# Decay rows inside the second score matmul, and compressed values at full height, in a two-layer hybrid decoder trunk

## The chip, the cores and the metric

The kernel runs on one core of a Trainium2 chip. The metric is device time in microseconds (us) for one execution. Three runs of the kernel before gave 987.95, 988.15 and 989.37 us; the median is 988.15.

## What is computed

Two layers on 512 tokens of width 1024, all in float32. Each layer normalises its input, projects it, and lets four token mixers work side by side: sparse attention (NSA: compressed, selected and window keys), pooling, a short convolution, and forgetting attention (Fox). Each result is gated, projected back to 1024, weighted by a merge gate, summed, and sent through an output projection onto the residual. The two parts that the change touches:

```python
# Fox: a score gets the difference of two cumulated log decays
logf = jax.nn.log_sigmoid(f_logit + f_bias)
c = jnp.cumsum(logf, axis=1)
s = jnp.einsum('bqhd,bkhd->bhqk', q_blk, k)
s = s + jnp.transpose(c_blk, (0, 2, 1))[..., None] - c_keys[:, :, None, :]
p = masked_softmax(s, (kpos[None, :] <= t[:, None])[None, None])
o = jnp.einsum('bhqk,bkhd->bqhd', p, v)
# NSA: attention over 31 compressed keys and values, four heads
s = jnp.einsum('bqhd,bnd->bhqn', q_blk, kc)
p_c = masked_softmax(s, (cmp_end[None, :] <= t[:, None])[None, None])
o_cmp = jnp.einsum('bhqn,bnd->bqhd', p_c, vc)
```

## The kernel before, in words

**Number format.** TensorE (PE) works on float32r, a rounded float32. Each operand is split into a high and a low part (`split`), and a product is three matmuls (high x high, high x low, low x high). ScalarE (ACT) makes the high part, VectorE (DVE) the low one.

**Dense products.** `dense` makes one 128-row output tile with 24 matmuls of 128x512. Its weights come from a list of 80 tiles per layer that `Stream` loads and splits ahead of their use. Each result leaves through a generator in `bg`, which is pumped one step after every second matmul.

**Score blocks.** `Unit.S(qt)` makes the scores of 128 queries against 128, 256, 384 or 512 keys. A head's query tile holds 64 rows of high part and 64 of low part (`q_stacks`); its key tiles hold the high part twice and the low part twice, one above the other (`k_stacks`, lines 284 to 295). So the first matmul (L565) gives (q high + q low) x k high, and the second (L566) (q high + q low) x k low. For the Fox heads a third one (L570) adds the decays. It has 32 rows, of which four are filled: keys hold the cumulated decay's high part, its low part, -1 and -1 (`state["cb"][0]`, in the buffer ropeC); queries hold 1, 1, the high part and the low part (`state["cb"][1]`, in ropeS). Each head has its own 32 rows, head h the rows from 32h. `decay` makes both tiles from `gz`.

**The rest of a block.** VectorE takes the minimum (the scores are negated; L573), ACT the exponential (L575), VectorE scales; `Unit.T` transposes on PE (L594), `split` takes that out to pth and ptl, and `Unit.PV` multiplies by the values (L615). For the first unit of each NSA head, `cmp_pv` opens the output with the compressed part: the transposed compressed probabilities of all four heads lie in one tile, 32 rows per head, and each head's matmul (L453) takes its 32 rows of it and of the compressed values `vc`, twice (high and low probabilities).

**Order.** Twelve units: for each of four heads a selected and a window unit (0 to 7), then four Fox heads (8 to 11). The loop runs 4 x 12 + 9 = 57 steps. A unit's four score blocks stand on its steps 0 to 3, its transposes on 4, 6 and 7, its value products on 7, 9 and 10. After each step `FILL` = 7 matmuls of the dense filler (Fox queries and keys, convolution, pooling, first merge gates) are put in. The framework then orders each engine's instructions; on the chip each engine takes its own in that order.

**Buffers.** The split queries and keys of a layer lie in 20 buffers called st: 4 of the NSA queries, 4 of the NSA keys, 4 of the Fox queries, 8 of the Fox keys. Weights use some of them before. Two PSUM buffers hold scores (ps_s), two hold transposes (ps_pt), one holds the output (ps_o).

Of the kernel before, what the change touches and what calls it, by code (L numbers as in the profile page):

```python
# [11 lines left out]
ALU = mybir.AluOpType  # L12
# [12 lines left out]
GATES = [(0, 0), (2, 0), (0, 1), (2, 1), (1, 0), (3, 0), (1, 1), (3, 1)]  # L25
BIG = 1e30
SWAP = [(i + 8) % 16 if i < 16 else i for i in range(32)]

# columns of the constant array
C_ID, C_TRI, C_MZ, C_CM, C_VAL, C_WINV, C_FIX, C_KCC, C_KCS, C_ROW = (  # L30
    0, 128, 256, 768, 896, 897, 899, 931, 963, 995)
NCONST = C_ROW + 6
# columns of the per-layer parameter array
P_B1, P_B2K, P_PSC, P_CW, P_POS, P_PW, P_W2K, P_W2V = 0, 2, 3, 5, 11, 43, 299, 427
# [5 lines left out]
def trunk_kernel(ctx: ExitStack, tc: tile.TileContext, xT, w_all, par_all, const, gains, rope, outT):  # L40
# [23 lines left out]
    def split(hi, lo, src, scale=None):  # L64
        """hi + lo = src (* scale), each in float32r."""
        if scale is None:
            ACT.activation(hi, src, AF.Copy)  # L67
            DVE.tensor_tensor(lo, src, f32(hi), ALU.subtract)  # L68
        else:
            ACT.activation(hi, src, AF.Copy, scale=scale)  # L70
            DVE.scalar_tensor_tensor(lo, src, scale, f32(hi), op0=ALU.mult, op1=ALU.subtract)  # L71

    # ---------------------------------------------------------------- constants
    cst = cpool.tile([128, NCONST], F32, name="cst")
# [5 lines left out]

    # ---------------------------------------------------------------- weights
    class Stream:
# [27 lines left out]
        def split(self, upto):  # L110
            while self.done <= min(upto, self.n - 1):
# [5 lines left out]
                if i == 2 or hid:  # L117
                    # slots that the stacks of q and k need only later
                    q = [sb([128, T], "st", 20, F32R) for _ in range(4)]
                    if hid:  # L120
                        for n in range(4):
                            v = q[n].rearrange("p (c two j) -> p c two j", two=2, j=128)
                            split(v[:, :, 0, :], v[:, :, 1, :],
                                  r[:, n * 256:n * 256 + 256].rearrange("p (c j) -> p c j", j=128))
                        self.parts[i] = q, None
                    else:
                        for n in range(2):
                            split(q[n], q[2 + n], r[:, n * 512:n * 512 + 512])
                        self.parts[i] = tuple(
                            [q[2 * j + k // 4][:, k % 4 * 128:k % 4 * 128 + 128] for k in range(8)]  # L130
                            for j in range(2))
                    self.load()
                    continue
# [27 lines left out]

    # ---------------------------------------------------------------- norm statistics
    def sum_squares(n, first, last):
        """add the squares gathered so far to the sums over the features"""
        if first:
            state["ssq"] = psum("o", 1)
        p, sq = state["ssq"], state["sq"]
        for tt in range(n // 128):
            PE.matmul(p[:, tt:tt + 1], sq[:, tt * 128:tt * 128 + 128], onesf[:, 0:1],  # L169
                      start=(first and tt == 0), stop=(last and tt == n // 128 - 1))  # L170
# [33 lines left out]

    # ---------------------------------------------------------------- dense products
    bg = []
# [15 lines left out]
    def dense(rhs, evac, tok=slice(0, T)):  # L222
        """one 128-row output tile: 8 contraction tiles, 3 passes"""
        i, (wh, wl) = ws.take()
# [27 lines left out]

    # ---------------------------------------------------------------- evacuations
    def scaled(acc):
# [26 lines left out]

    def k_stacks(dst, t):
        for o in (0, 64):
# [8 lines left out]
            yield  # L292
            ACT.activation(lo[e:e + 64], f32(lo[o:o + 64]), AF.Copy)
            dst.append((h, lo))
            yield

    # ---------------------------------------------------------------- compressed keys and values
    def ev_kcvc(acc):
# [81 lines left out]
    def cmp_v():  # L380
# [16 lines left out]
        yield  # L397
        vc = sb([128, 128], "vc", 1, F32R)
        split(vc[:, 0:64], vc[:, 64:128], r)
        state["vc"] = vc  # L400
# [49 lines left out]
    def cmp_pv(O, h):  # L450
        r = slice(32 * h, 32 * h + 32)
        for j, part in enumerate(state["pc"]):
            PE.matmul(O, state["vc"][r, :], part[r, :], start=(j == 0), stop=False,  # L453
                      tile_position=(32 * h, 0))

    # ---------------------------------------------------------------- values, gates of heads, decay
    def v_group(l):
# [90 lines left out]

    # ---------------------------------------------------------------- attention
    class Unit:  # L550
# [6 lines left out]
        def S(self, qt):  # L557
# [5 lines left out]
            s = psum("s", 2)  # L563
            qs = q[:, qt * 128:qt * 128 + 128]
            PE.matmul(s[:, :n], qs, kh[:, :n], start=True, stop=False)  # L565
            PE.matmul(s[:, :n], qs, kl[:, :n], start=False, stop=(self.head is None))  # L566
            if self.head is not None:
                r = slice(32 * self.head, 32 * self.head + 32)
                ck, cq = state["cb"]
                PE.matmul(s[:, :n], cq[r, qt * 128:qt * 128 + 128], ck[r, :n], start=False, stop=True,  # L570
                          tile_position=(32 * self.head, 0))
            nm, sm = sb([128, 1], "nm", 4), sb([128, 1], "sm", 4)
# [71 lines left out]

    # ---------------------------------------------------------------- conv and pool branches
    def ev_conv(kind, f):
# [79 lines left out]

    # ---------------------------------------------------------------- merge and output projection
    def ev_merge(i):
        # sigmoid(z) = (1 + tanh(z / 2)) / 2: tanh shares a function table with exp
        def g(acc):  # L730
            t = scaled(acc)
            state["sig"][i] = t
            yield
            ACT.activation(t, t, AF.Tanh, scale=0.5)  # L734
            yield
        return g
# [25 lines left out]

    # ================================================================ program
    nc.gpsimd.dma_start(ng, gains)
# [35 lines left out]
    for l in range(L):  # L800
        state["l"] = l
        state["gate"], state["y"], state["sig"] = {}, {}, {}
        Cp, Sp = sb([128, T], "ropeC", 1), sb([128, T], "ropeS", 1)
        nc.sync.dma_start(Cp, rope[0])
        nc.sync.dma_start(Sp, rope[1])
        rhs = (xh, xl)
        # first projections; the evacuation waits for the norm's statistics
        g0 = dense(rhs, ev_kcvc)
# [6 lines left out]
        run(g0)  # L815
        state["nk"], state["nq"], state["fq"], state["fk"] = [], [], [], []

        def ev_kskw(acc):
# [12 lines left out]
        def ev_fk(acc):  # L831
            t = scaled(acc)
            yield
            yield from k_stacks(state["fk"], t)

# [27 lines left out]

        # attention, with the remaining projections between its steps
        units = []
# [38 lines left out]
        for s in range(4 * len(units) + 9):  # L904
            for kind in ("PV", "T", "S"):
                for u in (s // 4 - 3, s // 4 - 2, s // 4 - 1, s // 4):
                    b = plan[kind].get(s - 4 * u)
                    if 0 <= u < len(units) and b is not None:
                        if kind == "S" and b == 0:
                            if u == 8:  # L910
                                while len(state["fk"]) < 4:
                                    next(fill)
                        getattr(units[u], kind)(b)
            for _ in range(FILL):
# [3 lines left out]

        # merge gates, branch projections
        ah, al = [], []  # L920
# [9 lines left out]

        # output projection and residual
        if l + 1 < L:
# [14 lines left out]

    # last layer: the tokens in two halves, so that the first one's norm and stores overlap
    xn = []
# [34 lines left out]

# [1 line left out]
def _constants(np):  # L986
# [11 lines left out]
    c[:, C_VAL] = p >= 31  # L998
    row = p % 32
    for j, v in enumerate(((0, 1), (2, -1), (1, 1), (2, 1), (0, 1), (3, 1))):  # L1000
        c[row == v[0], C_ROW + j] = v[1]
# [26 lines left out]
def _layout(np, a):  # L1028
# [8 lines left out]
    for l in range(L):  # L1037
# [7 lines left out]
        tiles = [feat(kv(0) + kv(1)), feat(kv(2) + kv(4)), feat(run(0)), feat(run(128))]  # L1045
        vc = kv(3) + kv(5) + list(range(2188, 2444)) + list(range(640, 652)) + list(range(2444, 2448))
        wv = w[:, vc].reshape(4, 2, 128, 400).transpose(0, 2, 1, 3).reshape(4, 128, 800)
# [29 lines left out]
        p[:, P_B2V:P_B2V + 64] = a["cmp_b2"][l, 1][None, :]  # L1077
        p[:, P_FB:P_FB + 4] = a["fox_f_bias"][l][None, :]
    return {"xT": a["x"][0].T, "w_all": w_all, "par": par, "const": c, "gains": ng, "rope": rope}
# [22 lines left out]
```

## Time and profile before

| | |
|---|---|
| median of three runs | 988.15 us (987.95 to 989.37) |
| the profiled execution, from its first to its last instruction | 987.6 us |
| PE busy | 970.9 us, 98%, 4824 matmuls |
| DVE, ACT, POOL busy | 653.6, 452.8, 12.9 us |
| granted TensorE clock, mean | 0.998 of full speed (2.4 GHz) |
| attention, first layer | about 110 to 262 us; its Fox scores 219 to 259 us |
| attention, second layer | about 590 to 748 us; its Fox scores 700 to 746 us |

The page shows one execution; it gives that one's span and no separate time. The span is 0.55 us below the median of the timed runs. Busy time counts an instruction's whole span. Matmuls overlap: their ends are modelled, and the distance between two starts is what the second one had to wait for the first.

### The profile page before, as it was taken

Reading aid. Unit: us, or ns where it says so; the run is one execution under the profiler, and the core shown is the slowest. Engines: PE = TensorE matmul, PEld = TensorE weight load, DVE = VectorE, ACT = ScalarE, POOL = GpSimd, SP = SyncE. Lnnn points to the kernel's source line nnn. Section 1 sums busy time; section 2 is a strip of 40 time slices with the busy share of each in tenths; the row PEclk is TensorE's granted clock in tenths of the full one; section 3 lists DMA queues with packets and bytes.
Section 4 is the critical chain, followed back from the end, with each engine's and each line's share of the span. In section 5 each row is a group of like instructions: output and inputs, shape, how many; then the busy total and the mean of one; then the engine's idle time right before and its main releaser. Section 6 shows DMA issues by size and latency. Waiting matters only on the chain.

```text
span 987.6 us, 12730 instructions
## 1 busy us (share of the span) xinstructions
PE 970.9 (98%) x4824; PEld 815.5 (83%) x4824; DVE 653.6 (66%) x1295; ACT 452.8 (46%) x800; POOL 12.9 (1%) x21
## 2 busy tenths in 40 slices
PE   7999999999999999999999999999999999999996
PEld 5988888887788888888889888888877888888896
DVE  6695699887675554446668549989668555454565
ACT  6294575555432322233427537555454323232363
POOL 0000000000000000000100000000000000000001
PEclk9999999999999999999999999999999999999999
DMA  6253221121213322334424322112111332323553
GB/s 257 77 172 105 86 85 62 47 98 32 75 65 111 103 95 98 97 117 169 166 67 160 124 89 83 65 65 64 65 43 43 107 103 89 107 86 107 171 193 128
DMA packets 31837, 100.62 MB, mean 102 GB/s; under 512 B 3600, under 2 KB 5664, under 8 KB 31776
## 3 DMA queue, kind: packets, MB, share of 16 engines
q1 hardware_dynamic: 30240, 96.65, 29.9%
q0 software_dynamic: 672, 2.11, 0.5%
q10 hardware_dynamic: 864, 1.05, 0.3%
q8 instruction: 38, 0.62, 0.3%
q14 instruction: 23, 0.19, 0.1%
HBM read 95.60 MB, written 4.19 MB: 101 GB/s over the span
## 4 chain that ended last, share of the span: by engine, by line
PE 98%; DVE 1%; DMA 0%; ACT 0%; issue 0%; POOL 0%; DVEq 0%; ACTq 0%; POOLq 0%
PE ps_d L235 72%; PE ps_s L749 4%; PE ps_pt L749 4%; PE ps_o L615 4%; PE ps_pt L594 3%; PE ps_s L469 2%; PE ps_pt L469 2%; PE ps_s L566 2%; PE ps_s L565 2%; PE ps_s L570 1%; PE ps_o L333 1%; PE ps_o L453 1%; DMA ng<-in_gains_dram 0%; PE ps_o L169 0%; ACT wh L67 0%; PE ps_s L411 0%
## 5 line engine op out<-in xcount | busy, mean ns | idle before, releaser
L235 PE MATMUL ps_d<-xh,wh 128*128 128x512 f32 x888 | 350.5, 395 | 7.8 <-ACT xh L70 6.9
L235 PE MATMUL ps_d<-xl,wh 128*128 128x512 f32 x888 | 349.7, 394 | 0.0
L67 ACT ACTIVATE wh<-wr 128x1024 fp32r<-128x1024 f32 (+2 forms) x160 | 166.8, 1044 | 345.1 <-issue 217.1
L235 PE MATMUL ps_d<-xh,wl 128*128 128x512 f32 x888 | 244.0, 392 | 0.0
L68 DVE TENSOR_TENSOR wl<-wr,wh 128x1024 fp32r<-128x1024 f32 (+2 forms) x160 | 192.6, 1204 | 52.9 <-ACT wh L67 42.8
L235 PEld LDWEIGHTS ps_d<-xh,wh 128*128 128x128 f32 x888 | 168.0, 189 | 42.6 <-ACT xh L70 6.9
L235 PEld LDWEIGHTS ps_d<-xl,wh 128*128 128x128 f32 x888 | 167.7, 189 | 34.2 <-DVE xl L71 1.2
L235 PEld LDWEIGHTS ps_d<-xh,wl 128*128 128x128 f32 x888 | 164.7, 188 | 33.9 <-issue 1.0
L256 DVE TENSOR_TENSOR t<-ps_d,rstd 128x512 f32<-128x512 f32 x106 | 73.0, 689 | 157.3 <-PE ps_d L235 156.9
L575 ACT ACTIVATE p<-p,nm 128x128 f32<-128x128 f32 (+1 forms) x96 | 53.4, 557 | 33.2 <-DVE nm L573 32.7
L235 PE MATMUL ps_d<-st,wh 128*128 128x256 f32 (+1 forms) x384 | 67.6, 319 | 0.8 <-ACT wh L67 0.8
L573 DVE CUSTOM_DVE_ANT_0 p<-ps_s,cst 128x128 f32<-128x128 f32 (+1 forms) x96 | 45.9, 486 | 33.1 <-PE ps_s L570 15.7
L235 PEld LDWEIGHTS ps_d<-st,wh 128*128 128x128 f32 x384 | 57.1, 190 | 6.1 <-ACT wh L67 1.0
L67 ACT ACTIVATE pth<-ps_pt 128x384 fp32r<-128x384 f32 (+1 forms) x72 | 37.7, 523 | 38.1 <-PE ps_o L615 21.2
L68 DVE TENSOR_TENSOR ptl<-ps_pt,pth 128x384 fp32r<-128x384 f32 (+1 forms) x72 | 42.6, 595 | 3.7 <-ACT pth L67 3.4
L749 PE MATMUL ps_pt<-y,wh 128*128 128x512 f32 x128 | 41.6, 391 | 0.0
L749 PE MATMUL ps_s<-y,wh 128*128 128x512 f32 x128 | 40.2, 393 | 0.3 <-DVE y L628 0.3
L594 PE MATMUL ps_pt<-cst,p 128*128 128x128 f32 x240 | 40.2, 277 | 0.0
L734 ACT ACTIVATE t<-t 128x512 f32<-128x512 f32 x64 | 39.4, 615 | 1.5 <-DVE t L256 1.5
L615 PE MATMUL ps_o<-pth,V 128*128 128x256 f32 x144 | 38.7, 283 | 0.0
L235 PE MATMUL ps_d<-st,wl 128*128 128x256 f32 (+1 forms) x192 | 37.9, 319 | 0.0
L615 PE MATMUL ps_o<-ptl,V 128*128 128x256 f32 x144 | 35.7, 290 | 0.0
(227 smaller groups left out, 1084.0 us busy)
## 6 DMA issues: line engine op xcount, KB each, us to landing
wr<-in_w_all_dram SPq DMA_DIRECT2D x159, 512.0 KB, 3.3
t<-in_xT_dram SPq DMA_DIRECT2D x16, 256.0 KB, 4.4
wr<-in_w_all_dram SPq DMA_DIRECT2D x8, 400.0 KB, 3.1
x1d<-t POOLq DMA_DIRECT2D x8, 256.0 KB, 2.3
xh<-x1d SPq DMA_DIRECT2D x8, 256.0 KB, 4.7
out_dram<-xh SPq DMA_DIRECT2D x12, 128.0 KB, 2.5
par<-in_par_dram SPq DMA_DIRECT2D x2, 279.5 KB, 4.8
wr<-in_w_all_dram ACTq DMA_DIRECT2D x2, 256.0 KB, 4.3
```

The lines of the kernel that those rows point to most:

```text
L67: ACT.activation(hi, src, AF.Copy)
L68: DVE.tensor_tensor(lo, src, f32(hi), ALU.subtract)
L235: PE.matmul(acc[:, :width], w, r[k][:, tok], start=(n == 0), stop=(n == 23))
L256: DVE.tensor_tensor(t, acc, state["rb"], ALU.mult)
L469: PE.matmul(accs[tt][:, 0:400], x[:, tt * 128:tt * 128 + 128], w, start=(k == 0 and a == 0), stop=(kp == 3 and kk == 1 and a == 2))
L565: PE.matmul(s[:, :n], qs, kh[:, :n], start=True, stop=False)
L573: DVE.tensor_tensor_reduce(out=P[:, :n], in0=s[:, :n], in1=bias, scale=1.0, scalar=3e38, op0=ALU.add, op1=ALU.min, accum_out=nm)
L575: ACT.activation(P[:, :n], P[:, :n], AF.Exp, bias=nm, scale=-1.0, accum_out=sm)
L594: PE.transpose(p[:, c:c + 128], self.P[qt][:, kb * 128:kb * 128 + 128], ident)
L615: PE.matmul(dst, V[:, kb, self.vset, :], part[:, src], start=(self.fresh and self.cmp is None and b == 0 and kb == 0 and j == 0), stop=(se ...
L734: ACT.activation(t, t, AF.Tanh, scale=0.5)
L749: PE.matmul(p, w[:, c], r, start=(n == 0), stop=(n == 5))
```

## The change

The decay rows move into the second Fox score matmul. The low part of a Fox key head now stands once (64 rows), and the other 64 rows of that tile hold the key decays of two heads, 32 rows each. A new generator, `q_decay`, makes a second query tile per Fox head: the 64 rows of the query's high part, the head's 32 rows of query decays, and 32 zero rows against the other head's decays. The second matmul (L586 now) uses that tile, and the third one goes. With this the product q low x k low is left out of the Fox scores. `HEAD_ROWS` orders the heads so that the decays of a head lie in the half of the tile that its query doesn't use.

The compressed values are made four times, each multiplied with a mask of one head's 32 rows, so `cmp_pv` multiplies all 128 rows and the other heads' rows are zero.

`q_decay` is put into `bg` at unit 6 (the Fox keys are finished first), and pumped to its end before unit 8's first score. Its fills run on GpSimd (POOL), its copies on ACT.

```diff
+HEAD_ROWS = (1, 3, 0, 2)
...
+C_HM = C_ROW + 6
+NCONST = C_HM + 4
...
-    def k_stacks(dst, t):
+    def k_stacks(dst, t, bias=False):
...
-            ACT.activation(lo[e:e + 64], f32(lo[o:o + 64]), AF.Copy)
+            ACT.activation(lo[e:e + 64], f32(state["cb"][0][e:e + 64] if bias else lo[o:o + 64]), AF.Copy)
...
+    def q_decay():
+        for h in range(4):
+            o, r = 64 * (h % 2), 32 * HEAD_ROWS.index(h)
+            z = r ^ 32
+            q2 = sb([128, T], "st", 20, F32R)
+            POOL.memset(f32(q2[z:z + 32]), 0.0)
+            ACT.activation(q2[o:o + 64], f32(state["fq"][h][o:o + 64]), AF.Copy)
+            yield
+            ACT.activation(q2[r:r + 32], f32(state["cb"][1][r:r + 32]), AF.Copy)
+            state["fq2"].append(q2)
+            yield
...
-        vc = sb([128, 128], "vc", 1, F32R)
-        split(vc[:, 0:64], vc[:, 64:128], r)
+        rm = sb([128, 4, 64], "vcm", 1)
+        DVE.tensor_tensor(rm, r.rearrange("p (o d) -> p o d", o=1).to_broadcast([128, 4, 64]),
+                          cst[:, C_HM:C_HM + 4].rearrange("p (h o) -> p h o", o=1).to_broadcast([128, 4, 64]),
+                          ALU.mult)
+        vc = sb([128, 4, 128], "vc", 1, F32R)
+        split(vc[:, :, 0:64], vc[:, :, 64:128], rm)
...
     def cmp_pv(O, h):
-        r = slice(32 * h, 32 * h + 32)
         for j, part in enumerate(state["pc"]):
-            PE.matmul(O, state["vc"][r, :], part[r, :], start=(j == 0), stop=False,
-                      tile_position=(32 * h, 0))
+            PE.matmul(O, state["vc"][:, h, :], part, start=(j == 0), stop=False)
...
-            qs = q[:, qt * 128:qt * 128 + 128]
-            PE.matmul(s[:, :n], qs, kh[:, :n], start=True, stop=False)
-            PE.matmul(s[:, :n], qs, kl[:, :n], start=False, stop=(self.head is None))
-            if self.head is not None:
-                r = slice(32 * self.head, 32 * self.head + 32)
-                ck, cq = state["cb"]
-                PE.matmul(s[:, :n], cq[r, qt * 128:qt * 128 + 128], ck[r, :n], start=False, stop=True,
-                          tile_position=(32 * self.head, 0))
+            c = slice(qt * 128, qt * 128 + 128)
+            q2 = q if self.head is None else state["fq2"][self.head]
+            PE.matmul(s[:, :n], q[:, c], kh[:, :n], start=True, stop=False)
+            PE.matmul(s[:, :n], q2[:, c], kl[:, :n], start=False, stop=True)
...
                         if kind == "S" and b == 0:
-                            if u == 8:
+                            if u == 6:
                                 while len(state["fk"]) < 4:
                                     next(fill)
+                                bg.append(q_decay())
+                            if u == 8:
+                                while len(state["fq2"]) < 4:
+                                    pump_bg(1)
```

The order of the instructions changes around this. First place: PE, first layer, the first score block of the first Fox head (128 columns). Before (ps_s are scores, ps_pt transposes, ps_o the output, ps_d a dense product):

```order
L594 MATMUL ps_pt<-cst,p 128x128 x3
L565 MATMUL ps_s<-st 128x128
L566 MATMUL ps_s<-st 128x128
L570 MATMUL ps_s<-ropeC,ropeS 128x128
L615 MATMUL ps_o<-pth,V 128x256
```

With the change:

```order
L609 MATMUL ps_pt<-cst,p 128x128 x3
L585 MATMUL ps_s<-st 128x128
L586 MATMUL ps_s<-st 128x128
L473 MATMUL ps_o<-ptc,vc 128x512 x2
L630 MATMUL ps_o<-pth,V 128x256
```

The third score row is gone, and nothing takes its place; the pair of compressed-value matmuls (L453 before, a few rows ahead of the block there) now stands right behind the scores. PE's dense matmuls between the blocks are the same ones, put elsewhere.

Second place: ACT, first layer, from the eviction of the compressed probabilities (ptc) on, at units 0 and 1. In brackets is what a row waits for. Before (p is an exponential, wh the high part of a weight tile, pth that of transposed probabilities):

```order
L67 ACTIVATE ptc<-ps_pt 128x512 [waits PE_49]
L67 ACTIVATE pth<-ps_pt 128x384 [waits PE_49]
L575 ACTIVATE p,sm<-p,nm 128x128 [waits DVE_49]
L67 ACTIVATE wh<-wr 128x1024 [waits DMAHW7_49,PE_49,Activation_49]
L575 ACTIVATE p,sm<-p,nm 128x256 [waits DVE_49]
L681 ACTIVATE t<-t 64x512 [waits DVE_49]
L67 ACTIVATE pth<-ps_pt 128x512 [waits PE_49]
L575 ACTIVATE p,sm<-p,nm 128x384 [waits DVE_49]
```

With the change:

```order
L69 ACTIVATE ptc<-ps_pt 128x512 [waits PE_49]
L69 ACTIVATE pth<-ps_pt 128x384 [waits PE_49]
L590 ACTIVATE p,sm<-p,nm 128x128 [waits DVE_49]
L590 ACTIVATE p,sm<-p,nm 128x256 [waits DVE_49]
L696 ACTIVATE t<-t 64x512 [waits DVE_49]
L307 ACTIVATE st<-st 64x512 [waits PE_49]
L309 ACTIVATE st<-ropeS 32x512
L69 ACTIVATE wh<-wr 128x1024 [waits DMAHW0_49,PE_49,Activation_49]
L590 ACTIVATE p,sm<-p,nm 128x384 [waits DVE_49]
```

The two copies of the first new query (L307, L309) stand six units ahead of their use, as soon as a buffer comes free: they wait for PE, and a weight split and the next exponential stand behind them. The other three queries of the layer follow in the same way at later units, each just ahead of the exponential of a unit's third or fourth score block.

## Rows read from the trace of the kernel before

**Rows 1.** The page, first part: busy time, share, instructions.
```profile
PE 970.9 (98%) x4824; PEld 815.5 (83%) x4824; DVE 653.6 (66%) x1295; ACT 452.8 (46%) x800; POOL 12.9 (1%) x21
```
**Rows 2.** The page, the chain that ended last: shares by engine.
```profile
PE 98%; DVE 1%; DMA 0%; ACT 0%; issue 0%; POOL 0%; DVEq 0%; ACTq 0%; POOLq 0%
```
**Rows 3.** Timeline, PE, Fox scores: start, length, engine, line, operation, shapes.
```profile
218.89 0.28 PE L566 MATMUL ps_s<-st 128*128 128x128 f32 x1
219.10 0.32 PE L570 MATMUL ps_s<-ropeC,ropeS 32*128 32x128 f32 x1
219.35 0.39 PE L615 MATMUL ps_o<-pth,V 128*128 128x256 f32 x1
219.57 0.28 PE L615 MATMUL ps_o<-ptl,V 128*128 128x256 f32 x1
...
258.10 0.39 PE L566 MATMUL ps_s<-st 128*128 128x512 f32 x1
258.42 0.49 PE L570 MATMUL ps_s<-ropeC,ropeS 32*128 32x512 f32 x1
258.84 0.50 PE L235 MATMUL ps_d<-xh,wh 128*128 128x512 f32 x1
259.18 0.39 PE L235 MATMUL ps_d<-xl,wh 128*128 128x512 f32 x1
```
**Rows 4.** Timeline, PE, scores of NSA units (without a decay matmul).
```profile
178.22 0.40 PE L566 MATMUL ps_s<-st 128*128 128x512 f32 x1
178.45 0.22 PE L565 MATMUL ps_s<-st 128*128 128x128 f32 x1
178.51 0.27 PE L566 MATMUL ps_s<-st 128*128 128x128 f32 x1
178.62 0.45 PE L235 MATMUL ps_d<-xh,wh 128*128 128x512 f32 x1
```
**Rows 5.** Line L570 alone: matmuls by form, and who waited (us, times).
```profile
L570 PE MATMUL ps_s<-ropeC,ropeS x32: 321/408/497, 219.1 to 745.6; 32*128 32x128 f32 x8, 32*128 32x256 f32 x8, 32*128 32x384 f32 x8, 32*128 32x512 f32 x8
...
  DVE p L573: 15.7, 13
```
**Rows 6.** Timeline, PE, around a pair of compressed-value matmuls.
```profile
168.18 0.39 PE L235 MATMUL ps_d<-xh,wh 128*128 128x512 f32 x1
168.50 0.73 PE L453 MATMUL ps_o<-ptc,vc 32*128 32x512 f32 x2
169.16 0.39 PE L615 MATMUL ps_o<-pth,V 128*128 128x256 f32 x1
169.38 0.28 PE L615 MATMUL ps_o<-ptl,V 128*128 128x256 f32 x1
169.50 0.22 PE L615 MATMUL ps_o<-pth,V 128*128 128x128 f32 x1
```
**Rows 7.** Busy time in two stretches: length, then each engine's busy us.
```profile
110.00:215.00 105.00, 105.00 (x549) 88.26 (x549) 95.46 (x242) 64.56 (x133) 0.00 (x0) 1.00 0.22 74
215.00:262.00 47.00, 47.00 (x240) 36.32 (x240) 32.58 (x94) 24.98 (x58) 0.00 (x0) 1.00 0.15 49
```
The engines stand in the order PE, PEld, DVE, ACT, POOL; then the granted clock, the DMA share and GB/s.

**Rows 8.** Single lines: ACT copy, DVE addition, POOL product; ns min/median/max.
```profile
L293 ACT ACTIVATE st<-st x12: 629/632/633, 54.0 to 614.4; 64x512 fp32r<-64x512 f32 x12
...
L418 DVE TENSOR_TENSOR p<-ps_s,t x4: 416/418/419, 112.2 to 593.3; 128x256 f32<-128x256 f32 x4
...
L979 POOL TENSOR_TENSOR xh<-xh,rstd x4: 722/820/930, 962.4 to 982.8; 128x256 f32<-128x256 f32 x4
```
**Rows 9.** Timeline, PE, behind the attention: idle before a matmul, and its releaser.
```profile
284.36 0.50 PE L235 MATMUL ps_d<-xh,wh 128*128 128x512 f32 x1 [0.47 <-ACT wh L67]
...
764.47 0.50 PE L749 MATMUL ps_s<-y,wh 128*128 128x512 f32 x1 [0.26 <-DVE y L628]
```

More of the change, by code (lines that the diff above doesn't have):

```diff
@@ L31 @@
     0, 128, 256, 768, 896, 897, 899, 931, 963, 995)
-NCONST = C_ROW + 6
+C_HM = C_ROW + 6
+NCONST = C_HM + 4
 P_B1, P_B2K, P_PSC, P_CW, P_POS, P_PW, P_W2K, P_W2V = 0, 2, 3, 5, 11, 43, 299, 427
@@ L802, in trunk_kernel @@
         state["gate"], state["y"], state["sig"] = {}, {}, {}
+        state.pop("cb", None)
         Cp, Sp = sb([128, T], "ropeC", 1), sb([128, T], "ropeS", 1)
@@ L816, in trunk_kernel @@
         state["nk"], state["nq"], state["fq"], state["fk"] = [], [], [], []
+        state["fq2"] = []
         def ev_kskw(acc):
@@ L833, in ev_fk @@
             yield
-            yield from k_stacks(state["fk"], t)
+            yield from k_stacks(state["fk"], t, bias=True)
         run(dense(rhs, ev_kskw))
@@ L999, in _constants @@
     row = p % 32
+    c[p, C_HM + p // 32] = 1
     for j, v in enumerate(((0, 1), (2, -1), (1, 1), (2, 1), (0, 1), (3, 1))):
@@ L1045, in _layout @@
         tiles = [feat(kv(0) + kv(1)), feat(kv(2) + kv(4)), feat(run(0)), feat(run(128))]
-        vc = kv(3) + kv(5) + list(range(2188, 2444)) + list(range(640, 652)) + list(range(2444, 2448))
+        vc = kv(3) + kv(5) + list(range(2188, 2444)) + list(range(640, 652)) + [2444 + h for h in HEAD_ROWS]
         wv = w[:, vc].reshape(4, 2, 128, 400).transpose(0, 2, 1, 3).reshape(4, 128, 800)
@@ L1077, in _layout @@
         p[:, P_B2V:P_B2V + 64] = a["cmp_b2"][l, 1][None, :]
-        p[:, P_FB:P_FB + 4] = a["fox_f_bias"][l][None, :]
+        p[:, P_FB:P_FB + 4] = a["fox_f_bias"][l][None, list(HEAD_ROWS)]
     return {"xT": a["x"][0].T, "w_all": w_all, "par": par, "const": c, "gains": ng, "rope": rope}
```

## The prediction

> **What bounds the kernel now.** Read the first part of the page first: TensorE (PE) is busy 970.9 of 987.6 us, 98%, the next engine is VectorE (DVE) with 66% [rows 1]. Then the chain of work that ended last: 98% of it is PE [rows 2], so what shortens PE's stream shortens the kernel, as long as nothing else takes its place. A busy share does not tell what one matmul costs, since their spans overlap (a 128x512 matmul lasts 0.39 us and the next starts 0.23 us later). The price is the distance from one start to the next in the timeline, which I call the pitch. In a stream of full-height matmuls the pitch goes with the columns: 512 columns 0.23 us (178.22 to 178.45), 128 columns 0.06 (178.45 to 178.51), or 0.11 where a wider matmul with new weights follows (178.51 to 178.62) [rows 4]; 256 columns 0.12 (169.38 to 169.50) [rows 6].
>
> Now the 32-row matmuls that the change removes. Around the decay matmul at 219.10 three pitches are too long, not one [rows 3]: the matmul before it takes 0.21 where 0.11 is usual, its own pitch is 0.25, and the one after it takes 0.22 where 0.12 is usual. Around the one of 512 columns at 258.42 the same: 0.32 for 0.23, 0.42 of its own, 0.34 for 0.23. The reader is to see that PE is never marked idle there: the loss hides in the overlapping spans, and only the starts show it. VectorE waited 15.7 us, 13 times, for just these decay matmuls [rows 5]: where it idles in that stage it waits for PE, not PE for it.
>
> **The change, part by part.**
>
> *32 decay matmuls go.* With 128 columns one costs (0.21 - 0.11) + 0.25 + (0.22 - 0.12) = 0.45 us, with 512 columns (0.32 - 0.23) + 0.42 + (0.34 - 0.23) = 0.62 us [rows 3, 4, 6]. Take off the columns' own 0.06 and 0.23 and both leave 0.39 us, so the entry to and exit from a 32-row matmul has a fixed price of 0.39. With 0.12 and 0.17 for 256 and 384 columns (between the rows of 128 and 512) those cost 0.51 and 0.56. There are eight of each width [rows 5]: 8 x (0.45 + 0.51 + 0.56 + 0.62) = 17.1 us. All of it lies on PE's path. The second score matmul stays at the same width; it only takes other weights, and it loaded its own weights before too. The first excerpt of the order shows that nothing stands in the removed rows' place.
>
> *16 compressed-value matmuls become full height.* They keep their 512 columns. A pair at 168.50 costs (0.32 - 0.23) before, 0.66 for the two in place of 2 x 0.23, and (0.22 - 0.12) behind: 0.39 us too much [rows 6], the same fixed price as above. In the order six pairs stand together and four matmuls stand alone in each version, so the fixed price is paid 6 + 4 = 10 times: 10 x 0.39 = 3.9 us. The rest of their cost stays.
>
> One rule speaks against both terms. What the rows show is that a 512-column matmul on 32 rows has a pitch of 0.42 us and one on 128 rows 0.23 [rows 3, 4]. The Trainium skill, TensorE: Matmul & The Clock Gate, sections "LDWEIGHTS" and "Why this matters for your kernels", says that a matmul of 32 rows takes as long as one of 128, and a 32-row weight load as long as a full one: height costs nothing. By that rule alone the second term would be nothing and the first only the columns; it is the second rival below, and I go by the rows.
>
> *What is added.* On ScalarE (ACT), per layer, four copies of 64x512 and four of 32x512 that build the new queries; a 64x512 copy takes 0.63 us [rows 8], and for the 32-row ones I take the same as an upper end: 5.0 us per layer, 10.1 in all. ACT is busy 64.6 of 105 us and 25.0 of 47 us in the two stretches in which they run [rows 7], so they lie beside PE's work. The four key copies per layer that now read the decay rows are as wide as the ones they replace; they no longer wait for VectorE's low part, but for the decay rows, which are made before them. On GpSimd (POOL) eight fills of 32x512: no such fill stands in the trace; a POOL operation of 128x256 takes 0.82 us [rows 8], a fill reads nothing, so between nothing and 0.82 each, on an engine with nothing else to do in this stage; only the fourth part of the new queries hangs on it, and these are read whole units later. I take nothing. On VectorE once per layer a 128x256 product, and the low part of 128x256 in place of 128x64; a 128x256 operation takes 0.42 [rows 8], so at most 0.84 us per layer, before 110 us, while PE works on the gate projections. Nothing. If that cover were gone it would be 1.7 us in all.
>
> *Waits.* Each new query takes a buffer that an older query or key leaves, so its copy waits in ACT's queue for PE (second excerpt). Behind it stand the exponentials, the evictions of transposed probabilities and the splits of weights. Four such waits per layer. Bounds: nothing, where PE has been there already, and one step of the attention, 152 us / 57 steps = 2.7 us [rows 7], where ACT stands for a whole step and PE then waits for it, 21 us in all. The nearest row is a wait of PE for VectorE by 0.26 us, and one for ACT by 0.47 [rows 9]. The copy comes just ahead of the exponential of the very score block for whose matmul it waits, which could not have run earlier either, so I take the small row, 0.26 us once per layer, 0.5 us.
>
> Sum: -17.1 - 3.9 + 0.5 = -20.5 us. Against the profiled execution's 987.6 us: 967.1. The median of the runs, 988.15, is 0.55 above that span; with it the forecast is **967.7 us**, 2.1% faster.
>
> **The rivals.**
>
> *VectorE and ACT take over the Fox stage.* In 215 to 262 us VectorE is busy 32.6 of 47 us [rows 7]. My first term takes 8.55 us per layer out of that stretch, to 38.5 us, of which VectorE would need 85%. The chain of a score block (minimum, exponential, reciprocal, scaling, transpose, split) would have less time per step. For it: in places the new order puts score blocks of 256 and 384 columns back to back. Against it: in 110 to 215 us VectorE runs at 95.5 of 105 us, 91%, and PE is not held up [rows 7]; and in the Fox stage VectorE waits for PE [rows 5]. If half of the term is given back there: 967.7 + 8.5 = 976.2 us.
>
> *Height is not what costs.* The gaps might belong to something that stays, say the change of query weights in the middle of an accumulation. Then the removal saves the columns alone, 8 x (0.06 + 0.12 + 0.17 + 0.23) = 4.6 us, and the compressed values nothing: 988.15 - 4.6 = 983.5 us. For it stands the rule named above. Against it: a full-height score pair without decay has the plain pitch [rows 4], and the compressed-value pairs, in quite other company, show the same 0.39 [rows 6].
>
> *Slower: the new queries stop ACT.* If a copy holds ACT for two steps, because the matmul that frees its buffer is itself behind transposes whose eviction stands behind the copy, PE waits about 5.4 us eight times, 43 us: 967.7 + 43 = 1011 us. It decides from 21 / 8 = 2.6 us per wait, about a whole step. For it: the waits are there in the order, and ACT takes its work strictly in turn. Against it: two score buffers let PE run one block ahead, a unit's transposes come three steps behind its scores, and ACT is idle 39% and 47% of the two stretches [rows 7].
>
> **How the numbers follow.** The forecast, 965.5 to 970: 0.75 (the lower end is the sum without waits, 967.2, less a pitch reading of 0.05 us on 32 matmuls; the upper end allows 2.3 us more waits, about 0.3 us for each new query). Given back in the Fox stage, 970 to 977: 0.14. Height is not what costs, 983.5: 0.05. Slower: 0.03. Below 965.5: 0.03. The range 965.5 to 976.5 reaches to the first rival. A measurement of this kernel tells 0.2%, 2.0 us, from no change. Faster by more than that: 0.95; within: 0.02; slower: 0.03.
>
> **What would show it.** PE should hold 4792 matmuls, no 32-row score and no 32-row ps_o<-ptc,vc. The pitch of the second score matmul should be 0.11, 0.12, 0.17 and 0.23 us by width, that of a compressed-value matmul 0.23. The Fox stage should be about 8.5 us shorter in each layer, and PE's idle time about what it was. It is wrong if PE shows gaps before score, transpose or weight matmuls in units 5 to 11, released by ACT (first and third rival), or if the second score matmul or its neighbours keep pitches 0.1 us too long (second).

## The result, and the profile after

The change takes 972.05 us (median of four runs, 971.83 to 972.54) against 988.05 of the kernel before on the same chip (987.80 to 989.37): the ratio is 0.9836, 95% interval 0.9822 to 0.9850, or 16.0 us. The forecast was 967.7 with a range of 965.5 to 976.5. So the sign and the range hold, and 4.4 us of the forecast gain are missing. The profiled execution spans 970.8 us, 16.8 less than the one before; in the runs below, a profiled execution's own time lies 1.7 to 2.1 us above its span.

First part of the page and shares of the chain that ended last, in the kernel after; they answer to [rows 1, 2]:

```profile
PE 951.2 (98%) x4792; PEld 809.7 (83%) x4792; DVE 654.9 (67%) x1297; ACT 460.7 (47%) x816; POOL 17.2 (2%) x29
...
PE 96%; DVE 2%; ACT 0%; DMA 0%; issue 0%; POOL 0%; DVEq 0%; ACTq 0%; POOLq 0%
```

32 matmuls are gone, and PE still sets the end, but its share of the chain fell from 98 to 96%: VectorE has come into it.

The pitches, in PE's timeline of the kernel after; they answer to [rows 3, 6] (L586 is the second score matmul, L473 the compressed values, L630 the values):

```profile
171.65 0.40 PE L237 MATMUL ps_d<-xl,wh 128*128 128x512 f32 x1
171.88 0.63 PE L473 MATMUL ps_o<-ptc,vc 128*128 128x512 f32 x2
172.35 0.28 PE L630 MATMUL ps_o<-pth,V 128*128 128x256 f32 x1
172.47 0.28 PE L630 MATMUL ps_o<-ptl,V 128*128 128x256 f32 x1
...
219.08 0.28 PE L586 MATMUL ps_s<-st 128*128 128x128 f32 x1
219.19 0.68 PE L473 MATMUL ps_o<-ptc,vc 128*128 128x512 f32 x2
...
221.74 0.28 PE L586 MATMUL ps_s<-st 128*128 128x256 f32 x1
221.85 0.34 PE L585 MATMUL ps_s<-st 128*128 128x384 f32 x1
222.03 0.34 PE L586 MATMUL ps_s<-st 128*128 128x384 f32 x1
222.21 0.28 PE L630 MATMUL ps_o<-pth,V 128*128 128x256 f32 x1
...
256.83 0.40 PE L586 MATMUL ps_s<-st 128*128 128x512 f32 x1
257.06 0.62 PE L764 MATMUL ps_s<-y,wh 128*128 128x512 f32 x2
```

The second score matmul now has a pitch of 0.11, 0.11, 0.18 and 0.23 us by width. The pair of compressed-value matmuls takes 0.47 (171.88 to 172.35) where it took 0.66, and what stands before and behind it keeps its plain pitch (0.23, 0.12). This part came as forecast.

The attention as a whole is shorter by 8.1 us in the second layer (161.4 to 153.3 us from its first score to its last value product), where PE does the same matmuls there less the sixteen decay matmuls; the forecast's parts make 10.5 (8.55 and half of 3.9). What came otherwise is the end of each attention. PE's timeline of the kernel after, the matmuls with idle time ahead of them behind the last Fox score of each layer, and what ended it (the row of 260.99 has none; it is the one that PE issued before it stood):

```profile
258.85 0.38 PE L630 MATMUL ps_o<-pth,V 128*128 128x256 f32 x1 [0.26 <-DVE o L654]
260.27 0.52 PE L609 MATMUL ps_pt<-cst,p 128*128 128x128 f32 x3 [0.58 <-DVE ptl L70]
260.99 0.28 PE L630 MATMUL ps_o<-pth,V 128*128 128x256 f32 x1
261.85 0.39 PE L630 MATMUL ps_o<-ptl,V 128*128 128x256 f32 x1 [0.58 <-DVE ptl L70]
273.64 0.50 PE L764 MATMUL ps_s<-y,wh 128*128 128x512 f32 x1 [0.26 <-DVE y L643]
275.29 0.50 PE L237 MATMUL ps_d<-xh,wh 128*128 128x512 f32 x1 [0.46 <-ACT wh L69]
...
731.98 0.39 PE L630 MATMUL ps_o<-pth,V 128*128 128x256 f32 x1 [0.16 <-DVE o L654]
733.45 0.30 PE L609 MATMUL ps_pt<-cst,p 128*128 128x128 f32 x1 [0.63 <-DVE ptl L70]
734.90 0.44 PE L609 MATMUL ps_pt<-cst,p 128*128 128x128 f32 x2 [0.68 <-DVE p L600]
747.23 0.50 PE L764 MATMUL ps_s<-y,wh 128*128 128x512 f32 x1 [0.29 <-DVE y L643]
748.88 0.50 PE L237 MATMUL ps_d<-xh,wh 128*128 128x512 f32 x1 [0.46 <-ACT wh L69]
```

Before, only three of these stood there: the wait for wh behind the branch projection, in both layers (in the second at 766.11, 0.44 us), and the one for y in the second [rows 9]. The others are new: PE waits for the low part of transposed probabilities (ptl), for a scaled score block (p L600), for a head's output to be taken from its buffer (o), and in the first layer for y. The marked idle time is 3.2 us more than before. By starts it is more, since a matmul's modelled span covers the first part of a wait: from 260.99 to 261.85 PE stood 0.86 where the pitch is 0.12. Counted that way the six waits for ptl, p and o are 4.0 us, about 2.0 per layer, and the new one for y adds 0.4.

In the Fox stage itself nothing is lost. Busy time of PE, PEld, DVE, ACT and POOL in two stretches of the kernel after; the first answers to [rows 7]:

```profile
215.00:253.00 38.00, 38.00 (x218) 33.15 (x218) 29.52 (x85) 21.99 (x53) 0.00 (x0) 1.00 0.20 64
258.00:276.00 18.00, 15.87 (x82) 12.40 (x81) 15.64 (x30) 7.60 (x14) 0.00 (x0) 1.00 0.10 30
```

VectorE needs 78% of the stage and PE has no gap; behind the last score VectorE works 15.6 of 18 us, and PE waits.

Why there? The order of PE tells it. Number of dense matmuls (ps_d) between points of the attention, first layer and second layer:

```
                            first score  unit 4    unit 8    unit 10    last score
                            to unit 4    to 8      to 10     to last    to last value
                                                             score      product
before                      160, 160     144, 143  43, 49    35, 62     42, 10
the change                  186, 186     139, 140  51, 40    48, 58      0,  0
before + key decays         186, 186     139, 140  48, 46    41, 28     10, 24
change without key decays   161, 161     143, 142  48, 49    48, 71     24,  1
change + one dense tile     186, 186     139, 140  50, 48    60, 64     13, 10
before + one dense tile     160, 160     144, 143  48, 49    48, 62     48, 34
```

The filler is the same 424 matmuls per layer, 448 with the extra tile. In the change 26 of them moved to before unit 4, the shorter Fox stage took the rest, and none is left for the time in which the last unit's scores go through minimum, exponential, scaling, transpose and split.

### The profile page after: what moved, and what is told of

The parts are those of the page before. It is cut to its first block, busy times and chain, and to the rows that moved or that the text cites. A ratio compares the mean times of both kernels' runs of the same rounds, so it can differ in the third digit from the quotient of the medians.

```text
span 970.8 us, 12716 instructions
## 1 busy us (share of the span) xinstructions
PE 951.2 (98%) x4792; PEld 809.7 (83%) x4792; DVE 654.9 (67%) x1297; ACT 460.7 (47%) x816; POOL 17.2 (2%) x29
## 4 chain that ended last, share of the span: by engine, by line
PE 96%; DVE 2%; ACT 0%; DMA 0%; issue 0%; POOL 0%; DVEq 0%; ACTq 0%; POOLq 0%
PE ps_d L237 73%; PE ps_s L764 4%; PE ps_pt L764 4%; PE ps_o L630 3%; PE ps_pt L609 3%; PE ps_s L488 2%; PE ps_pt L488 2%; PE ps_s L586 2%; PE ps_s L585 1%; PE ps_o L349 1%; DVE t L769 1%; DMA ng<-in_gains_dram 0%; PE ps_o L171 0%; PE ps_o L473 0%; PE ps_o L199 0%
## 5 line engine op out<-in xcount | busy, mean ns | idle before, releaser
L237 PE MATMUL ps_d<-xh,wl 128*128 128x512 f32 x888 | 241.2, 391 | 0.0
L630 PE MATMUL ps_o<-pth,V 128*128 128x256 f32 x144 | 37.3, 275 | 0.4 <-DVE o L654 0.4
L630 PE MATMUL ps_o<-ptl,V 128*128 128x256 f32 x144 | 36.1, 292 | 0.6 <-DVE ptl L70 0.6
```

What stands on the lines that cost most here:

```text
L237: PE.matmul(acc[:, :width], w, r[k][:, tok], start=(n == 0), stop=(n == 23))
L630: PE.matmul(dst, V[:, kb, self.vset, :], part[:, src], start=(self.fresh and self.cmp is None and b == 0 and kb == 0 and j == 0), stop=(se ...
```

## Experiments

The theory after the result: the two prices hold (a fixed 0.39 us per entry to and exit from 32 rows), and 4 us are given back because the filler is used up before the last unit is through. Rivals: that height is not what costs; that the new copies and their waits cost the 4 us; that the end of the attention is slow whatever the filler.

**The decay part alone.** `cmp_pv` and `vc` as before, everything else as changed:

```diff
...
     def cmp_pv(O, h):
+        r = slice(32 * h, 32 * h + 32)
         for j, part in enumerate(state["pc"]):
-            PE.matmul(O, state["vc"][:, h, :], part, start=(j == 0), stop=False)
+            PE.matmul(O, state["vc"][r, :], part[r, :], start=(j == 0), stop=False,
+                      tile_position=(32 * h, 0))
```

> The change without its compressed-value part: cmp_pv keeps its 32-row matmuls, the decays ride in the second score matmul. Theory (a 32-row matmul costs a fixed 0.39 us beside its columns, and some 4 us are given back at the end of the two attention stages, where the dense filler has run out): 988.1 - 17.1 + about 4 = 975 us, 3.9 us above the whole change; the ten entries and exits of L453 keep their long pitches. Rival (height is not what costs): 983.5 us.

Measured: 976.36 us against 988.86 before on that chip, ratio 0.9878 (0.9863 to 0.9893), 12.5 us faster. Waits of PE behind the last scores as in the whole change. The rival's 983.5 is out.

**The compressed values alone.** The kernel before, with the masks and `cmp_pv` of the change:

```diff
...
     def cmp_pv(O, h):
-        r = slice(32 * h, 32 * h + 32)
         for j, part in enumerate(state["pc"]):
-            PE.matmul(O, state["vc"][r, :], part[r, :], start=(j == 0), stop=False,
-                      tile_position=(32 * h, 0))
+            PE.matmul(O, state["vc"][:, h, :], part, start=(j == 0), stop=False)
...
```

> The kernel before with the compressed values at full height alone. Theory: ten times 0.39 us, 984.2 us, and since the Fox stage keeps its length no new waits of PE at the end of the attention. Rival (height is not what costs): 988.1 us.

Measured: 984.71 us against 988.86, ratio 0.9959 (0.9945 to 0.9973): 4.15 us, where 3.9 had been forecast. No new waits. The two parts, 12.5 and 4.15, make 16.65, close to the 16.0 of the whole.

**The third score matmul at full height.** The kernel before; only the rows change:

```diff
-                r = slice(32 * self.head, 32 * self.head + 32)
                 ck, cq = state["cb"]
-                PE.matmul(s[:, :n], cq[r, qt * 128:qt * 128 + 128], ck[r, :n], start=False, stop=True,
-                          tile_position=(32 * self.head, 0))
+                PE.matmul(s[:, :n], cq[:, qt * 128:qt * 128 + 128], ck[:, :n], start=False, stop=True)
```

> The kernel before, but the third score matmul takes all 128 rows of the two decay tiles in place of one head's 32. This adds the decays of all four heads to each head's scores, so the numbers are not the reference's. The 32 matmuls and their columns stay, only the height changes. Theory: the fixed price goes, 32 x 0.39 = 12.5 us, of which 1 to 3 us may be given back at the end of the attention: 975.6 to 978.6 us. Rival (height is not what costs): 988.1 us.

Measured: 977.15 us against 988.86, ratio 0.9881 (0.9866 to 0.9896), 11.7 us faster with the same number of matmuls and columns. PE's timeline of this kernel at the first Fox block (L569 is the third score matmul):

```profile
218.31 0.28 PE L566 MATMUL ps_s<-st 128*128 128x128 f32 x1
218.42 0.28 PE L569 MATMUL ps_s<-ropeC,ropeS 128*128 128x128 f32 x1
218.53 0.33 PE L613 MATMUL ps_o<-pth,V 128*128 128x256 f32 x1
218.70 0.28 PE L613 MATMUL ps_o<-ptl,V 128*128 128x256 f32 x1
```

0.11, 0.11 and 0.17 us, where the 32-row matmul had 0.21, 0.25 and 0.22 [rows 3]. The price of the height is 11.7 / 32 = 0.37 us; the interval of the run leaves 0.32 to 0.41, so my 0.39 is not contradicted. This kernel keeps the order of the kernel before, 42 and 10 dense matmuls behind the last score; its Fox stage is shorter by some seven tenths (11.7 of 16.3 us) of what the change takes out, and it has no wait of PE there that the kernel before lacks.

**The change without its new query tiles.**

```diff
-            q2 = q if self.head is None else state["fq2"][self.head]
+            q2 = q
...
-                                bg.append(q_decay())
...
```

> The change without the new query tiles: the second Fox score matmul takes the first one's query tile, so the decays are left out (the low halves that now meet decay rows are noise), and the eight fills on GpSimd, the sixteen copies on ScalarE and their waits are gone; PE's matmuls are the same. Theory (the 4 us that are missing are lost because PE reaches the end of the attention sooner than the chain of the last units allows): 972 us, within 1 us of the change, with the same waits of PE behind the last scores. Rival (the copies and their waits in ScalarE's queue cost it): 968 us and no such waits.

Measured: 974.07 us against 988.86, ratio 0.9849 (0.9834 to 0.9864): no faster than the change, and 2 us above the 972 that I expected. The fastest of its four runs took 972.25 us; the profiled one, 975.21, is among the longer executions of the last section. PE's timeline of this kernel shows the same waits:

```profile
261.39 0.52 PE L609 MATMUL ps_pt<-cst,p 128*128 128x128 f32 x3 [0.58 <-DVE ptl L70]
262.96 0.39 PE L630 MATMUL ps_o<-ptl,V 128*128 128x256 f32 x1 [0.58 <-DVE ptl L70]
...
734.50 0.30 PE L609 MATMUL ps_pt<-cst,p 128*128 128x128 f32 x1 [0.63 <-DVE ptl L70]
```

So the copies are not what costs, though ScalarE did stand for them. In the kernel after, the copy L307 with what ended the idle time ahead of it (us, times), and the fill L306:

```profile
L307 ACT ACTIVATE st<-st x8: 628/632/634, 138.4 to 679.6; 64x512 fp32r<-64x512 f32 x8
...
  PE ps_s L586: 10.3, 4
...
L306 POOL MEMSET st<- x8: 515/520/575, 138.5 to 678.6; 32x512 f32 x8
```

Ahead of four of the eight copies ScalarE stood 2.6 us each on average, a whole step of the attention. PE lost nothing by it: without the copies it has the same waits.

**The change once more.** The same kernel, on the chip of the next ones.

> The change once more, beside the next three on the same chip: 0.9836 of the kernel before, with the same waits of PE behind the last scores of each layer.

Measured: 973.89 us (971.95, 972.45, 975.33 and 975.38) against 988.34, ratio 0.9851 (0.9836 to 0.9866). The waits are the same. Where two of its runs lose 3 us is told in the last section.

**The change without key decays.** Same matmuls on PE, another order of the filler:

```diff
-            yield from k_stacks(state["fk"], t, bias=True)
+            yield from k_stacks(state["fk"], t)
```

> The change, but the Fox key tiles hold the low part twice as before, so no key decays are added and the query decays meet key low parts: the decays are left out. PE's matmuls are the same; the order differs: between the last score and the last value product PE has 24 dense matmuls left in the first layer and 1 in the second, where the change has 0 and 0. Theory (PE waits at the end of the attention because its dense filler has been used up earlier): the waits of the first layer go, those of the second stay, about 2 us faster than the change. Rival (the chain of the last units is slow whatever the filler): no faster than the change, waits in both layers.

Measured: 970.55 us against 988.34, ratio 0.9817 (0.9803 to 0.9830), 1.5 us faster than the change's first median and 3.3 than its median on this chip, where 2 had been expected; each of its runs is below each run of the change. Where 24 dense matmuls are left, in the first layer, the new waits are gone. Where one is left, PE still waits, 1.0 us of marked idle time, but at another place: ahead of a branch projection, for y, which comes from the output of a head. So the second layer bears the theory out in the sum and not in the kind of wait. PE's idle time at the end of the two attentions in this kernel (the first row, behind the branch projection, stood there before [rows 9]; the two rows of the second layer are new):

```profile
273.85 0.50 PE L237 MATMUL ps_d<-xh,wh 128*128 128x512 f32 x1 [0.46 <-ACT wh L69]
...
733.32 0.96 PE L764 MATMUL ps_s<-y,wh 128*128 128x512 f32 x3 [0.86 <-ACT y L641]
735.90 0.50 PE L764 MATMUL ps_s<-y,wh 128*128 128x512 f32 x1 [0.15 <-DVE y L643]
...
```

**One dense tile more in the filler.** The change, with the first merge gate of the next output tile ahead of each branch projection, in the program and in the list of weights:

```diff
...
             for i in range(4):
-                yield from dense(rhs, ev_merge(i))
+                yield from dense(rhs, ev_merge(0, i))
+            yield from dense(rhs, ev_merge(1, 0))
...
-                for i in range(4):
-                    run(dense(rhs, ev_merge(i)))
+                for i in range(1, 4):
+                    run(dense(rhs, ev_merge(m, i)))
+                if m < KT - 1:
+                    run(dense(rhs, ev_merge(m + 1, 0)))
...
-            tiles += [feat(run(3472 + 1024 * i + 128 * m)) for i in range(4)]
+            tiles += [feat(run(3472 + 1024 * i + 128 * m)) for i in range(1 if m else 0, 4)]
+            if m < 7:
+                tiles.append(feat(run(3472 + 128 * (m + 1))))
```

> The change with one dense tile more in the filler: the first merge gate of the second output tile (24 matmuls) moves ahead of the first branch projection, with its place in the list of weights, and so for every later tile. Nothing is left out. The order then has 13 and 10 dense matmuls behind the last score. Theory (filler used up): most of the 3.7 us of waits come back, 3 to 4 us faster than the change, about 0.980 of the kernel before. Rival (the chain is slow whatever the filler): the waits move by the length of the tile and stay; no faster than the change.

Measured: 968.38 us (968.09 to 968.60) against 988.34, ratio 0.9796 (0.9783 to 0.9810): faster than the change, by 3.7 us against its first median and 3.6 against its best run beside it. What is left of PE's idle time there:

```profile
277.71 0.50 PE L764 MATMUL ps_s<-y,wh 128*128 128x512 f32 x1 [0.29 <-DVE y L643]
279.36 0.50 PE L237 MATMUL ps_d<-xh,wh 128*128 128x512 f32 x1 [0.45 <-ACT wh L69]
...
749.01 0.50 PE L764 MATMUL ps_s<-y,wh 128*128 128x512 f32 x1 [0.31 <-DVE y L643]
750.66 0.50 PE L237 MATMUL ps_d<-xh,wh 128*128 128x512 f32 x1 [0.45 <-ACT wh L69]
```

All waits for ptl, p and o are gone; three of these four stood in the kernel before as well.

**The same tile in the kernel before.** The same edit on the old code.

> The kernel before with the same dense tile moved ahead. There PE waits only about 1.5 us at the end of both attention stages, since 42 and 10 dense matmuls stand behind the last score. Theory (filler used up): at most 1.5 us faster, so the tile helps the change more than the kernel before. Rival (the moved tile is a gain of its own): as much faster as in the changed kernel, 3 to 4 us.

Measured: 989.93 us against 988.34, ratio 1.0014 (1.0005 to 1.0023): 1.6 us slower, where I had expected it up to 1.5 faster. Part of that shows as two waits that the kernel before does not have:

```profile
287.92 0.50 PE L749 MATMUL ps_s<-y,wh 128*128 128x512 f32 x1 [0.43 <-DVE y L628]
...
760.59 0.50 PE L749 MATMUL ps_s<-y,wl 128*128 128x512 f32 x1 [0.52 <-DVE wl L68]
```

The tile is no gain of its own; it helps where the filler is missing.

**The key decays alone in the kernel before.** Which piece moves the filler forward?

```diff
...
-            ACT.activation(lo[e:e + 64], f32(lo[o:o + 64]), AF.Copy)
+            ACT.activation(lo[e:e + 64], f32(state["cb"][0][e:e + 64] if bias else lo[o:o + 64]), AF.Copy)
...
```

> The kernel before with one piece of the change: the upper or lower half of a Fox key's low tile takes the key decays in place of a second copy of the low part, while the third score matmul stays (so decays are counted with wrong queries, and the numbers are not the reference's). PE's matmuls are the same. In the order this piece alone moves 26 dense matmuls from behind unit 4 to ahead of it, as in the change, and leaves 10 and 24 behind the last score (before: 42 and 10). Theory (the filler that has moved forward costs only where it runs out, in the change, whose Fox stage is shorter): within 1.5 us of the kernel before, and no waits of PE behind the last scores beyond its own. Rival (the earlier copies themselves cost time): slower by 2 us or more.

Measured: 989.35 us against 988.25, ratio 1.0008 (0.9999 to 1.0017). The order has the 186 of the change, and the time is 1.1 us longer, which its interval does not tell from none; one new wait of 0.52 us, which I had not expected, stands in the first layer:

```profile
273.83 0.50 PE L749 MATMUL ps_s<-y,wl 128*128 128x512 f32 x1 [0.52 <-DVE wl L68]
```

Moving the filler costs little by itself: here 10 and 24 dense matmuls are still left behind the last score. In the change, where the stage behind it is shorter too, none is.

**The extra tile, and the next weight split issued earlier.** Against the kernel with the extra tile:

```diff
...
         i0, (wh, wl) = ws.take()
+        ws.split(i0 + 1)
...
-            if i == 0:
-                ws.split(i0 + 1)
```

> The change with the extra dense tile in the filler, and the split of the weights behind a branch projection issued ahead of that projection instead of inside it. Nothing is left out. If the remaining wait of 0.62 us for ScalarE's high part behind the first branch projection of each layer is one of order, it goes: 967 us, 1.2 us faster than with the extra tile alone. Rival (it waits for the buffer): no difference, 968.4 us.

Measured: 968.57 us against 988.25, ratio 0.9795 (0.9779 to 0.9811): no difference, as the rival said. The trace of this kernel shows what the remaining 0.45 us goes back to: the weight split on ACT has itself stood 1.73 us for a matmul of the branch projection (L765), as it does with the extra tile alone. That fits a wait for a weight buffer; no run frees one to test it.

```profile
278.51 2.01 ACT L69 ACTIVATE wh<-wr 128x1024 fp32r<-128x1024 f32 x2 [1.73 <-PE ps_s L765]
```

## Why the prediction was right in range and 4.4 us off

- *32 decay matmuls go, 17.1 us.* Right in kind, and in size as far as the runs tell: the third matmul at full height gives a fixed price of 0.37 in place of 0.39, a difference within its interval. With 0.37 and the columns' 4.6 us the term is 16.3.
- *16 compressed-value matmuls, 3.9 us.* Right: 4.15 measured alone.
- *Height is not what costs* (0.05). Refuted by the third matmul at full height and by both parts alone. The rule of the Trainium skill cited with it (TensorE: Matmul & The Clock Gate, "Why this matters for your kernels": a matmul of 32 rows takes as long as one of 128) speaks of a single matmul, which no run here isolates. For one on 32 rows within a full-height stream it does not give the time: there the height cost 0.37 us each.
- *What is added, nothing.* Right: without the query copies the kernel is no faster. A 32x512 fill takes 0.52 us on POOL, and the 32x512 copy as long as the 64x512 one.
- *The step that failed: "Waits", "I take the small row, 0.26 us once per layer, 0.5 us".* I looked for waits at the new copies. There ScalarE did wait, 10.3 us, and it cost PE nothing. The waits that cost, 4.0 us and 0.4 for y, stand at and behind the end of the attention, released by VectorE. Two of my signs speak of it: PE's idle time was to stay about what it was, and gaps ahead of scores or transposes were to show a rival, but ones released by ACT. I had the order in hand and said of it that the dense matmuls are the same ones, put elsewhere; I did not count how many are left behind the last score. With 20.4 us of gain (16.3 + 4.15) less 4.4 the sum is 16.0, and 16.0 was measured; each of these differences has an interval of some 1.4 us to either side, so the exact agreement is luck.
- *VectorE and ACT take over the Fox stage, 976.2* (0.14). The time missed the forecast's own band (965.5 to 970, 0.75) and lies in the band given to this rival; that the range holds it at all is owed to the rival. But the mechanism is another: in the stage PE is not held up. It is the chain of the last unit, which VectorE carries, with nothing left on PE to cover it.
- *Slower: the new queries stop ACT.* ScalarE's waits are as long as PE's would have had to be for that rival to break even (2.6 us), but only four of the eight copies waited, and PE ran on.

## What to carry to other kernels

In this kernel a matmul on 32 rows between full-height ones cost 0.37 us beyond its columns, which are worth 0.06 to 0.23. If the rows can be padded with zeros or ride in another matmul, compare the distance of starts, not the busy time. And when PE time is taken out of a stage that ends in a dependent chain, count the independent matmuls that the new order leaves behind the last link. Here the shorter stage and the filler that moved forward together left none and opened waits at its end; either alone cost nothing that is clear of noise, and one tile of later work moved ahead closed the waits.

## What was not expected of the hardware

Two kernels, the change and the one without query copies, showed executions some 3 us longer than others of the same kernel; the decay part alone had one of 2.4 us (978.52 us), of which there is no trace. Busy time and granted clock (the number behind POOL's) in two stretches, first an execution of 975.38 us of the change:

```profile
732.30:736.30 4.00, 2.53 (x17) 1.69 (x16) 3.94 (x11) 2.85 (x9) 0.00 (x0) 1.00 0.41 131
...
737.00:740.00 3.00, 3.00 (x10) 2.46 (x9) 1.47 (x4) 0.80 (x2) 0.00 (x0) 0.50 0.00 0
```

and one of 972.54 us, in the same place of the program, which it reaches 1.3 us earlier:

```profile
731.00:735.00 4.00, 2.53 (x17) 1.69 (x16) 3.94 (x11) 2.85 (x9) 0.00 (x0) 1.00 0.39 131
...
736.00:739.00 3.00, 3.00 (x20) 2.56 (x19) 2.44 (x5) 1.09 (x2) 0.00 (x0) 1.00 0.00 0
```

In both, PE had been busy 2.53 of 4 us in the waits of the second layer, with no single marked gap over 0.7 us. Behind them the clock fell to 1.2 GHz in the one, for some 3 us, and stayed at 2.4 GHz in the other; what decides between the two, no run shows. From the last score to the last value product that is 14.2 us in place of 12.6. The rest of the 3 us lies at the start, where the first score comes 1.3 us later in the slower of the two. So the waits cost the change more in some executions than in others; the four runs of the kernel with the extra tile lay within 0.6 us.
